# Loading the first half of the first token tile as one DMA, with most constants behind it and the weight loads gated on it

## The chip, the cores and the metric

The kernel runs on the eight cores of one Trainium2 chip; each core computes its own share of the tokens, and the cores do not wait for each other. The metric is the device time of the slowest core in microseconds (us), lower is better. A core's **span** is the time from its first to its last instruction in the trace. Some executions fall into a slower state of the chip, in which the cores of one die (cores 0 to 3 or 4 to 7) show a lower clock; times are compared between fast runs only. The **granted clock** is the share of the TensorE clock that the traces show as let through; "half clock" below means a granted clock of 0.5.

## The reference, cut to what matters

One layer of a decoder: 8 prompts of 2064 tokens (16 of them learned), 128 running sequences with one token each, 1024 channels. The part that matters here is the very beginning: a normalization and a first matrix product.

```python
def rmsnorm(x, g):
    xf = x.astype(jnp.float32)
    y = xf * lax.rsqrt(jnp.mean(xf * xf, axis=-1, keepdims=True) + EPS)
    return (y * g.astype(jnp.float32)).astype(x.dtype)

def trunk_layer(x, ...):
    h = rmsnorm(x, g_pre_mix)
    z = h @ w_in                       # 1024 -> 4096 columns
    u, v, bg, cg, ga, gb = jnp.split(z, IN_SPLITS, axis=-1)
    ...                                # pooling mixer, gated conv mixer, gated FFN
```

## The kernel before: the parts concerned

The tokens of a core are cut into tiles. Channels lie on the partitions: tile 0, called x0, has 8 "rows" of 128 channels by 512 tokens in float32, 256 KB each. The matrix product starts on unnormalized rows (`RAW` = x times the gain), and the normalization factor is multiplied in afterwards; it comes from a sum of squares, which is a matmul with a matrix of equal values (`ONES`). The engines' order is made by a list scheduler from the operations below; `after=` holds a DMA's issue back until another DMA has landed.

```python
def warm(n):                           # fillers: matmuls without a use, they keep the clock up
    pe([(bank(6, 128), ONES, ONES)] * n, [ONESB.t()], [("ps", 6)], 128)

PARTS0 = ((0, 2), (2, 2), (4, 2), (6, 1), (7, 1))          # (first row, rows) of each DMA of x0
for q, (k, m) in enumerate(PARTS0):
    xs0.append(sp_dma(X[0].flat[...], xT[0][k // 2][...], ...))
    if q == 0:
        sp_dma(CST, cst, [], [KCST], 128 * 256 * 4, ...)   # all constants, behind the first piece
...
warm(60)
for i in range(16):
    wload(W_IN, w_in, i, after=[xs0[1 if i else 0]])       # block 0 after piece 0, the others after piece 1
# ... w_pool, w_in 16 to 31, w_co: after=[xs0[1]]
for q in range(4):                                         # tile 1, in four quarters
    pool_dma(X[1].flat[...], xT[1][q], ..., after=[xs0[1]])

for k, m in PARTS0:
    act(... AF.Square ...)                                 # ScalarE: squares of a piece
    for r in range(k, k + m):
        dve(... tensor_scalar, scalar1=cc(C_G1 + k) ...)   # VectorE: RAW, needs the constants
for k, m in PARTS0:
    if k == 6:
        win_group(0, 0, b0, F_lo(0, 0), RAW[0], 0, 6)      # first w_in matmuls, 500 columns
    pe([(bank(SB, N0), ONES, XSQ2[0].ap[:, r, :]) for r in range(k, k + m)], ...)   # sums of squares
    if k < 4:
        warm(20)
# ... five blocks of w_in on tile 0, 512 columns; then tile 1, 392 columns
```

The weight loads (`wload`) and the load of tile 1 are issued by GpSimd, one after the other: eight blocks of w_in, then the four quarters of tile 1, then the next blocks. Each issue takes GpSimd about 0.7 us, the first of a series 0.9.

## Time and profile before

| what | before | from |
|---|---|---|
| time, median of 3 runs | 809.15 us (808.97 to 810.61) | the times |
| span, slowest and fastest core | 809.3 and 806.4 us | cores view |
| TensorE (PE) busy | 98% of the span | profile page |
| first x0 piece (512 KB) lands, mean of 8 cores | 5.20 us | start of the table load on ScalarE |
| tile 1 asked for, mean of 8 cores | 14.39 us | start of GpSimd's `big<-xT` row |
| first scaling of tile 1 by ScalarE, mean | 28.18 us | ScalarE's 128x392 row |
| first matmul on tile 1 (T1), mean and latest | 30.19 and 32.04 us | PE's first 392-column row |

The first line of the profile page:

```profile
span 809.3 us, 15144 instructions; the slowest of 8 cores (806.4 to 809.3 us)
```

PE is the bound, and only its first 60 us differ between cores, so the argument is about the start-up. The next fence is the timeline of core 2, a core that the prediction does not show. Columns: start, length, engine and line, what is read and written, count, and in brackets the idle time before it and what ended that.

```profile
5.24 0.90 POOL L515 DMA_DIRECT2D big<-w_in  x1 [3.89 <-DMA big<-xT]
...
9.77 5.13 POOL L515 DMA_DIRECT2D big<-w_in  x7 [3.63 <-DMA big<-xT]
...
14.89 2.22 POOL L515 DMA_DIRECT2D big<-xT  x4
...
17.70 12.00 PE L502 MATMUL ps<-big 128*128 128x500 bf16 x56 [1.67 <-DMA big<-w_in]
...
28.11 0.59 ACT L694 ACTIVATE big<-ps 128x500 f32<-128x500 f32 x1 [2.34 <-PE ps L502]
...
28.59 0.61 ACT L1049 ACTIVATE big<-big 128x392 bf16<-128x392 f32 x1
```

GpSimd asks for one w_in block when the first piece of x0 has landed, then idles 3.63 us until the second piece has, then asks for seven blocks, and then for tile 1. PE meanwhile waits 1.67 us for block 1. The last two lines are ScalarE's: it first evacuates a block of tile 0 (L694), for which it has waited for PE, and only then scales tile 1 (L1049). PE idles 0.91 to 1.13 us at T1 on every core. This order of ScalarE is the list scheduler's choice.

### The profile page before, as it was taken

Reading aid. Unit: us, or ns where it says so; the run is one execution under the profiler, and the core shown is the slowest. Engines: PE = TensorE matmul, PEld = TensorE weight load, DVE = VectorE, ACT = ScalarE, POOL = GpSimd, SP = SyncE. Lnnn points to the kernel's source line nnn. Section 1 sums busy time; section 2 is a strip of 40 time slices with the busy share of each in tenths; the row PEclk is TensorE's granted clock in tenths of the full one; section 3 lists DMA queues with packets and bytes.
Section 4 is the critical chain, followed back from the end, with each engine's and each line's share of the span. In section 5 each row is a group of like instructions: output and inputs, shape, how many; then the busy total and the mean of one; then the engine's idle time right before and its main releaser. Section 6 shows DMA issues by size and latency. Waiting matters only on the chain.

```text
span 809.3 us, 15144 instructions; the slowest of 8 cores (806.4 to 809.3 us)
## 1 busy us (share of the span) xinstructions
PE 794.6 (98%) x4514; PEld 439.9 (54%) x4518; DVE 557.4 (69%) x971; ACT 431.6 (53%) x813; POOL 251.7 (31%) x268
## 2 busy tenths in 40 slices
PE   6999999999999999999999999999999999999996
PEld 4445445555555555555555555555555555577664
DVE  2897438796986778478899555665567655675656
ACT  3434284765565546576655444644446444565552
POOL 6542002001201133589534321342223422242124
PEclk9999999999999999999999999999999999999999
DMA  9999704756105989997952983382122721159644
GB/s 182 199 164 159 156 1 113 194 151 132 63 23 115 193 150 204 167 162 101 199 163 47 161 170 101 79 157 75 66 77 59 157 80 68 69 103 252 210 154 176
DMA packets 76255, 106.29 MB, mean 131 GB/s; under 512 B 12400, under 2 KB 65776, under 8 KB 76160
## 3 DMA queue, kind: packets, MB, share of 16 engines
q0 software_dynamic: 38992, 43.11, 37.3%
q1 hardware_dynamic: 37184, 62.22, 24.3%
q8 instruction: 39, 0.64, 0.3%
q14 instruction: 40, 0.33, 0.2%
HBM read 106.98 MB, written 28.67 MB: 168 GB/s over the span
## 4 chain that ended last, share of the span: by engine, by line
PE 96%; DMA 2%; DVE 1%; issue 0%; ACT 0%; DVEq 0%; ACTq 0%; POOLq 0%
PE ps L502 96%; DMA big<-w_in 1%; DMA big<-xT 1%; DVE big L582 0%; DVEq L1168 0%; ACT big L1049 0%; DVE big L691 0%; ACT big L570 0%; DVE big L697 0%; ACT big L972 0%; ACT big L954 0%; ACT big L974 0%; ACTq L273 0%; DVE big L978 0%; ACT big L694 0%
## 5 line engine op out<-in xcount | busy, mean ns | idle before, releaser
L502 PE MATMUL ps<-big 128*128 128x392 bf16 (+9 forms) x4514 | 794.6, 339 | 8.1 <-ACT big L1028 2.4
L502 PEld LDWEIGHTS ps<-big 128*128 128x128 bf16 x4518 | 439.9, 98 | 362.5 <-issue 11.9
L856 DVE SCALAR_TENSOR_TENSOR big<-ps,big 128x456 f32<-128x456 f32 (+2 forms) x440 | 268.8, 639 | 103.8 <-ACT big L852 78.9
L870 POOL TENSOR_TENSOR big<-big 128x448 bf16<-128x448 f32 (+2 forms) x110 | 118.5, 1079 | 267.6 <-DVE big L856 165.7
L852 ACT ACTIVATE big<-ps,big 128x448 f32<-128x448 f32 (+2 forms) x220 | 128.9, 599 | 69.4 <-PE ps L502 65.0
L869 ACT ACTIVATE big<-big 128x448 f32<-128x448 f32 (+2 forms) x110 | 60.1, 547 | 52.3 <-DVE big L856 50.7
L733 ACT ACTIVATE big<-ps 128x392 f32<-128x392 f32 (+1 forms) x80 | 39.5, 513 | 58.9 <-PE ps L502 36.2
L513 POOL DMA_DIRECT2D big<-xT x16 | 14.9, 943 | 164.0 <-DVE big L746 150.5
L887 ACT ACTIVATE big<-ps,big 128x448 f32<-128x448 f32 (+1 forms) x32 | 20.4, 637 | 68.2 <-PE ps L502 68.1
L515 POOL DMA_DIRECT2D big<-w_up x44 | 31.9, 726 | 55.0 <-PE ps L502 46.8
L746 DVE SCALAR_TENSOR_TENSOR big<-ps,big 128x392 f32<-128x392 f32 (+1 forms) x40 | 25.8, 645 | 31.9 <-PE ps L502 29.3
L542 DVE TENSOR_TENSOR big<-big 128x1568 bf16<-128x1568 bf16 (+3 forms) x28 | 23.7, 850 | 29.8 <-ACT big L765 29.2
L893 DVE TENSOR_TENSOR big<-big 128x896 bf16<-128x896 bf16 (+1 forms) x12 | 7.6, 630 | 37.2 <-ACT big L890 37.2
L763 ACT ACTIVATE big<-ps,big 128x392 f32<-128x392 f32 (+1 forms) x40 | 24.5, 612 | 14.2 <-PE ps L502 14.1
L639 DVE TENSOR_TENSOR big<-big 128x406 f32<-128x406 f32 (+7 forms) x50 | 29.8, 597 | 1.5 <-ACT big L661 0.2
L582 DVE SCALAR_TENSOR_TENSOR big<-big 128x392 bf16<-128x392 f32 (+1 forms) x40 | 24.2, 645 | 8.1 <-ACT big L559 5.3
L515 POOL DMA_DIRECT2D big<-w_in x32 | 23.2, 752 | 19.3 <-DMA big<-w_in 8.9
L608 ACT ACTIVATE big<-big 128x392 f32<-128x392 f32 (+1 forms) x20 | 12.7, 637 | 29.1 <-DVE big L697 29.1
L817 DVE SCALAR_TENSOR_TENSOR big<-big 128x392 bf16<-128x392 f32 (+1 forms) x40 | 27.1, 710 | 0.8 <-ACT big L556 0.8
L611 DVE SCALAR_TENSOR_TENSOR big<-big 128x392 f32<-128x392 f32 (+1 forms) x40 | 25.4, 641 | 2.6 <-ACT big L608 2.1
L752 DVE TENSOR_TENSOR big<-big 128x392 bf16<-128x392 f32 (+1 forms) x40 | 24.8, 630 | 2.0
L750 DVE TENSOR_TENSOR big<-ps,big 128x392 f32<-128x392 f32 (+1 forms) x40 | 23.3, 583 | 1.9 <-PE ps L502 0.6
(68 smaller groups left out, 345.8 us busy)
## 6 DMA issues: line engine op xcount, KB each, us to landing
big<-w_dnb SPq DMA_DIRECT2D x32, 704.0 KB, 4.6
big<-w_up POOLq DMA_DIRECT2D x44, 256.0 KB, 10.2
big<-w_in POOLq DMA_DIRECT2D x32, 256.0 KB, 22.0
big<-xT POOLq DMA_DIRECT2D x16, 392.0 KB, 6.9
big<-w_dn POOLq DMA_DIRECT2D x8, 704.0 KB, 10.2
w_dnb<-big SPq DMA_DIRECT2D x8, 704.0 KB, 6.4
big<-xT SPq DMA_DIRECT2D x6, 784.0 KB, 6.7
yT<-big SPq DMA_DIRECT2D x6, 784.0 KB, 6.4
```

The costliest lines, as they stand in the source:

```text
L502: ins = e.matmul(o, lhsT=l, rhs=x, start=(start and i == 0), stop=(stop and i == last))
L515: return S.add("pool", lambda e: e.dma_start(out=out, in_=in_, max_dma_last_dim=mx), r, w, dma=True, byts=byts, pri=pri, after=after)
L611: dve(lambda e, k=k: e.scalar_tensor_tensor(out=cv, in0=p[:, 2 + k + lo:2 + k + N], scalar=cc(C_WC + 4 * k + c), in1=cv, op0=ALU.mult, op1 ...
L639: dve(lambda e, nx=nx, cur=cur, s=s, a2=a2: e.tensor_tensor(out=nx[:, a2:W], in0=cur[:, a2:W], in1=cur[:, a2 - s:W - s], op=ALU.add), [ct] ...
L733: act(lambda e, b=b, g=g: e.activation(out=GT[t].ap[:, g, lo:N], in_=bank(b, N, lo), func=AF.Sigmoid), [("ps", b)], [GT[t].t(g, 1)], N, ps ...
L746: dve(lambda e: e.scalar_tensor_tensor(out=A_, in0=bank(bp, N, lo), scalar=cc(C_PS + m), in1=A_, op0=ALU.mult, op1=ALU.mult), [("ps", bp), ...
L752: dve(lambda e: e.tensor_tensor(out=MERGED[t].ap[:, m, lo:N], in0=A_, in1=B_, op=ALU.add), [G_.t(ga, 1), G_.t(gb, 1)], [MERGED[t].t(m, 1)], N)
L817: dve(lambda e: e.scalar_tensor_tensor(out=h, in0=r, scalar=cc(C_G3 + k), in1=SD.ap[:, rs, lo:N], op0=ALU.mult, op1=ALU.mult), [R[t].t(k, ...
L852: act(lambda e, b=b, fj=fj, tt=tt: e.activation(out=tt[:, 0:n], in_=bank(b, n), func=AF.Copy, scale=cc(C_WF + fj)), [("ps", b), KCST], [to ...
L856: dve(lambda e, b=b, fj=fj, tt=tt, k=k: e.scalar_tensor_tensor(out=tt[:, 0:n], in0=ps[:, b * 512 + k:b * 512 + k + n], scalar=cc(C_WF + 44 ...
L869: act(lambda e: e.activation(out=g, in_=g, func=AF.Silu), [T.t(0, 1)], [T.t(0, 1)], N, tab="silu")
L870: S.add("pool", lambda e: e.tensor_tensor(out=gb.ap[:, j, 0:N], in0=g, in1=v, op=ALU.mult), [T.t()], [gb.t(j, 1)], dur=N * 2.17 + 100)
```

## The change

Its intent: fetch x0 in fewer and longer DMAs (four rows, 1 MB, first; contiguous runs of 8 KB instead of 4 KB), let only the 8 constant columns that the start needs go in front and the rest behind, and ask for all weights as soon as that first piece has landed. The fillers between the sums are 10, 10 and 20 in place of 20 and 20, and the length that the list scheduler assumes for the first fillers is set by hand. Cut to its core:

```diff
+PARTS0 = ((0, 4), (4, 2), (6, 2))          # layout of x0 in DRAM
-    PARTS0 = ((0, 2), (2, 2), (4, 2), (6, 1), (7, 1))
-        if q == 0:
-            sp_dma(CST, cst, [], [KCST], 128 * 256 * 4, pri=-2e6 + 2e4)
+    sp_dma(CST[:, 0:8], cst[:, 0:8], [], ["cg1"], 128 * 8 * 4, pri=-2.1e6)
+    LD0 = ((0, 4), (4, 2), (6, 1), (7, 1))
+    for q, (k, m) in enumerate(LD0):
+        xs0.append(sp_dma(X[0].flat[...], x0p[j][...], ...))
+    sp_dma(CST[:, 8:256], cst[:, 8:256], [], [KCST], 128 * 248 * 4, pri=-1.8e6)
...
     for i in range(16):
-        wload(W_IN, w_in, i, after=[xs0[1 if i else 0]])
+        wload(W_IN, w_in, i, after=[xs0[0]])
     # the same for w_pool, w_co, w_o, the other blocks and tile 1: xs0[1] -> xs0[0]
...
-        if k < 4:
-            warm(20)
+            if r < 6:
+                warm(10 if r < 4 else 20)
```

## The prediction

> **What bounds the kernel now.** I read the cores view first, then the timeline of the first 34 us core by core, then the chain of waits, then the windows view for the clock.
>
> ```profile
> core 0: 806.7 us, clock 0.998
> ...
> core 4: 809.3 us, clock 0.997
> core 5: 806.4 us, clock 0.998
> ```
>
> The slowest core sets the time, and the cores differ by 3 us. The windows view says where: from 60 to 800 us PE is busy all the time on every core (200.00 of 200 us in nearly every stretch), so the difference is made before 60 us. In the timelines I take the start of the first matmul group with 392 columns (the second token tile) as a marker, called T1. It is 29.13 us on core 0, 32.04 on core 4, 29.01 on core 5, and 30.65, 30.60, 30.32, 30.43, 29.36 on cores 1, 2, 3, 6, 7. Span minus T1 is 777.6, 777.3, 777.4 for the first three and 777.0 to 777.6 for all eight. So **span = T1 + 777.3 us**, and the change can act on the time only through T1 of the slowest core. Core 4's timeline, PE and ScalarE rows (start, busy time, then in brackets the idle time before and its releaser):
>
> ```profile
> 1.41 5.45 PE L502 MATMUL ps<-big 128*128 128x128 bf16 x60 [1.41 <-POOL big L1011]
> ...
> 5.87 1.28 ACT L1028 ACT_TABLE_LOAD   x1 [5.87 <-DMA big<-xT]
> 7.16 1.06 ACT L1028 ACTIVATE big<-big 128x1024 bf16<-128x1024 f32 x1
> 8.58 3.23 PE L502 MATMUL ps<-big 128*128 128x512 bf16 x43 [1.72 <-ACT big L1028]
> ...
> 12.51 0.59 PE L502 MATMUL ps<-big 128*128 128x512 bf16 x2 [0.70 <-ACT big L1028]
> ...
> 15.33 2.28 PE L502 MATMUL ps<-big 128*128 128x500 bf16 x6 [2.23 <-DMA big<-w_in]
> ...
> 32.04 2.15 PE L502 MATMUL ps<-big 128*128 128x392 bf16 x12 [0.91 <-ACT big L1049]
> ```
>
> PE warms up on 60 fillers, then waits for the squares of x0, then for w_in block 0, which lands at 15.2 us though it was issued at 6.45. The rows of 8 by 512 columns that follow (56 matmuls) take 12.0 us. Then PE idles 0.91 us at T1; on every core it is 0.91 to 1.13 us, because ScalarE scales rows of tile 1 only after it has evacuated a block that PE has just finished. On cores 2, 3, 6 and 7 there is a second DMA wait, for w_in block 1, of 0.9 to 1.7 us. The clock on core 4 (last three columns: granted clock, DMA share, GB/s):
>
> ```profile
> 15.00:15.50 0.50, 0.17 (x1) 0.13 (x2) 0.00 (x0) 0.00 (x0) 0.50 (x2) 1.00 0.95 139
> 15.50:16.00 0.50, 0.50 (x3) 0.23 (x2) 0.00 (x0) 0.00 (x0) 0.50 (x2) 0.75 1.14 158
> 16.00:16.50 0.50, 0.50 (x2) 0.15 (x1) 0.00 (x0) 0.00 (x0) 0.50 (x2) 0.50 1.08 174
> ...
> 19.00:19.50 0.50, 0.50 (x3) 0.24 (x2) 0.00 (x0) 0.41 (x2) 0.50 (x1) 0.84 1.16 176
> ```
>
> Read the clock column: half speed from about 15.75 (0.75 is half of the slice) to 19.16 us, 3.4 us in all, which costs 1.7 us of matmul time. Core 1 has the same from about 14.25 to 17.05. The other six have none. So core 4 is slowest because its w_in block came last and because it was throttled.
>
> **What the skill says.** The Trainium skill, "TensorE: Matmul & The Clock Gate", Part 1, describes a gate that halves the PE clock after an idle window of about 3.4 us, free-running against the kernel. The length agrees with the 3.41 us above. The trigger is looser here: the window before core 4's drop (12.33 to 15.75) held 0.59 + 0.42 us of PE work, 30%; the one before core 1's held about 42%. On core 7 a window with about 51% did not trip it. I work with "under half busy". The skill, "ScalarE: Activation LUTs", What ACT_TABLE_LOAD costs, gives 1283 ns; the trace has 1.28 us, and it starts only when the first x0 piece has landed. The skill, "Perfetto Trace Analysis", DMA Optimizations, says that growing small DMA runs to 4 or 8 KB raises throughput. This trace cannot show 8 KB, but it shows a dip: on core 4 115 GB/s in the half microsecond after 6.0 us, between 332 and 215, about when the constants in 1 KB rows pass; every core has one. The skill, "DMA: Bandwidth & Descriptors", Specifications, says that pieces below 512 B are read, modified and written. That bears on the new 32-byte rows of constants; no row of this trace shows it.
>
> **The change part by part.**
>
> x0 pieces. Before: 512 KB first, landing at 4.66 to 5.87 us over the cores, 1.18 MB (with the constants) at 7.5 to 9.5. After: a 4 KB piece, then 1.05 MB as one DMA. The extra issue costs 0.43 us (mean issue time in the timeline). Summing the GB/s column, 1.05 MB had moved by 5.6 to 6.95 us, the constants' dip in it. Take 0.4 for the dip off and 0.43 for the issue on, add the lag from moved to landed (0.5 to 1.4 us on the first piece, 1.0 to 2.6 on the second): the piece A of four rows **lands at about 7.6 us**, 7.0 to 8.5.
>
> First square. It now waits for A. Table load 1.28 + square 1.06 + 0.15 of semaphores: first sum matmul at 7.6 + 2.5 = 10.1 us, against 8.58 on core 4 and about 7.4 to 8.0 on the others. Fillers end at 6.33 to 7.68 (1.41 plus 4.92 to 6.27). So the first PE gap **grows from about 1.1 to about 3 us**. That is my chosen point of danger: nearly every position of a 3.4 us window over such a gap has a window under half busy (core 4's 5.7 to 9.1 would hold 1.2 us, 35%).
>
> Fillers and sums at half clock. A sum pair of 512 columns takes 0.86 us instead of 0.43, ten fillers 1.07 instead of 0.56. From 10.1: pair 10.96, ten 12.03, pair 12.9, ten 13.96, pair 14.8, twenty at most 17.0. The clock returns after a window full of work, between 13.1 and 16.5 by the core's phase, so the last part runs fast: **the first w_in matmul starts at 15.1 to 16.7 us** (before: 13.2 to 15.3). At full clock it would be 13.75.
>
> w_in block 0. Issued at A + 0.6, with 0.9 for the first issue, so it enters at 9.1 us with some 0.3 to 0.5 MB of x0 and constants before it. It reads 0.52 MB at about 320 GB/s (the column shows about 160 GB/s written as bf16, half the bytes read), so 1.6 + 1.3 + about 2 of lag: about 14. Block 1 follows some 1.7 us later, ahead of its use, so the second DMA wait of cores 2, 3, 6 and 7 goes.
>
> To T1. From the first w_in matmul: 6 matmuls, the last two sums and 2 matmuls 2.2 us at full clock, 56 matmuls 12.0, idle 0.91: 15.1 us. So T1 = 30.2 to 31.8, slowest core about 31.4 against 32.04. There is a floor: the second quarter of tile 1 lands at about 28 us (ScalarE picks it up at 28.26 to 28.38 on the fast cores), its scaling makes T1 about 29.0. Bytes ahead of it are unchanged, so it stays near 28.
>
> Constants. The remaining ones land at 11 to 11.5 us, first needed for the logarithm's bias after 15 us: no cost. Sum: 0.6 us less on the slowest core, **808.7 us** by 777.3 + 31.4; I take reported time and slowest span as equal (809.15 and 809.3).
>
> **The rivals.** First: the intended gain. If A lands early, or PE is not throttled in the gap, the first w_in matmul starts when block 0 lands, at 13.8 to 14.3 us, with no wait for block 1 and no half clock later. T1 is then 29.0 to 29.8, the last by the floor, and the time about 806.9. For it: every part removes a wait that some core shows, and x0 no longer shares the DMA engines with w_in. Against: the gap above. Second: the throttle lasts longer. On a core whose phase makes the half clock last to 16.5 us and whose A lands after 8.2, the whole sequence moves to 17.5 us and T1 to 32.6 or more: about 810. For it: eight cores with free phases make the worst case likely on one of them. Third: the DMA stream is the limit in any case; T1 of cores 0 and 5 already sits at its floor of 29.0, so nothing below 806.3 can be had without loading tile 1 earlier.
>
> **Range and chances.** Weights of 0.55 for the main line (808.7), 0.3 for the intended gain (806.9) and 0.15 for the longer throttle (810) give 808.4. The runs before lie over 1.6 us by themselves. I predict **808.4 us, range 806.5 to 810.2**. Two per cent are 16 us, more than the whole start-up that can be affected, so within 2% has 0.98 and each side 0.01.
>
> **What would show it right or wrong.** Right: the table load starts at 7.0 to 8.5 us; the PE gap after the 60 fillers is 2.5 to 3.5 us; the clock column falls to 0.5 on most cores between 8 and 12 us and is back at 1.0 by 17; no PE wait for w_in block 1; span minus T1 still 777.3 within 0.4. Wrong, towards faster: the clock stays at 1.0 through the gap, and the first w_in matmul waits for its DMA at 13.5 to 14.5. Wrong, towards slower: T1 above 32.5 on some core, or a DMA wait for tile 1 in front of T1, which would mean that the stream got slower. If span minus T1 moves by more than 0.5, the scheduler has reordered something later and my one-marker account fails.

## More of the kernel before

Stretches of 1 us on core 1, from the windows view; the last three columns are the granted clock of PE, the DMA share and GB/s (a packet is counted whole in the stretch where it starts, so a share can be over 1):

```profile
3.00:4.00 1.00, 1.00 (x12) 1.00 (x11) 0.00 (x0) 0.00 (x0) 0.00 (x0) 1.00 0.72 221
4.00:5.00 1.00, 1.00 (x13) 1.00 (x11) 0.00 (x0) 0.00 (x0) 0.00 (x0) 1.00 0.92 343
...
12.00:13.00 1.00, 0.59 (x2) 0.13 (x2) 0.78 (x3) 1.00 (x3) 1.00 (x2) 1.00 1.21 192
13.00:14.00 1.00, 0.06 (x1) 0.09 (x2) 0.20 (x1) 0.33 (x1) 1.00 (x2) 1.00 1.16 179
```

The DMA engines are busy in all four of them (these stretches answer to those shown of the changed kernel below).

## The result, and the profile after

The four runs after took 812.05, 810.82, 895.97 and 864.37 us. The last two are in the slow state (a die at clock 0.89 to 0.96). Executions in which one die ran at a lower clock are left out of the means. The kernel before, its three runs with a fourth taken beside these, had a median of 809.48 us (808.97 to 810.61). The ratio of fast runs is 1.0022 with a 95% interval of 0.9998 to 1.0046: the same within 2%, and rather slower than faster. Ratios here are the mean time of one kernel's fast runs over that of the other's in the same rounds, so not quite the ratio of the medians that are quoted. Both fast runs lie above the predicted 808.4 us and above the upper end of the range, 810.2 us.

Cores view after:

```profile
core 0: 807.7 us, clock 0.997
core 1: 810.5 us, clock 0.994
...
core 4: 809.3 us, clock 0.993
```

Core 1 is now the slowest, and both it and core 4 have a lower clock than any core before. The timeline of core 1:

```profile
1.41 5.39 PE L504 MATMUL ps<-big 128*128 128x128 bf16 x60 [1.41 <-POOL big L1019]
...
10.22 1.28 ACT L1039 ACT_TABLE_LOAD   x1 [10.22 <-DMA big<-x0a]
10.80 6.04 POOL L517 DMA_DIRECT2D big<-w_in  x8 [9.45 <-DMA big<-x0a]
...
12.71 10.59 PE L504 MATMUL ps<-big 128*128 128x512 bf16 x72 [5.91 <-ACT big L1039]
16.81 2.24 POOL L517 DMA_DIRECT2D big<-xT  x4
...
24.53 8.63 PE L504 MATMUL ps<-big 128*128 128x500 bf16 x40 [1.24 <-DMA big<-w_in]
...
31.25 0.62 ACT L1062 ACTIVATE big<-big 128x392 bf16<-128x392 f32 x1 [1.52 <-DMA big<-xT]
...
33.42 2.81 PE L504 MATMUL ps<-big 128*128 128x392 bf16 x16 [0.26 <-ACT big L1062]
```

The 1 MB piece lands at 10.22 us. PE has run out of fillers at 6.80 and waits 5.91 us for the first square. GpSimd asks for the first weights at 10.80 and for tile 1 at 16.81. Before T1, which is 33.42 us here, ScalarE waits 1.52 us for tile 1 to land. The chain of waits of the same core names the same pieces (start, length, what):

```profile
1.51 8.63 DMA big<-x0a
...
10.80 6.01 POOL big L517 x8
16.81 14.36 DMA big<-xT
```

Loading x0, issuing eight weight loads and fetching tile 1 follow each other without slack. The windows view of core 1:

```profile
3.00:4.00 1.00, 1.00 (x12) 1.00 (x11) 0.00 (x0) 0.00 (x0) 0.00 (x0) 1.00 1.20 106
4.00:5.00 1.00, 1.00 (x13) 1.00 (x11) 0.00 (x0) 0.00 (x0) 0.00 (x0) 1.00 0.49 123
...
9.00:10.00 1.00, 0.00 (x0) 0.00 (x0) 0.00 (x0) 0.00 (x0) 0.00 (x0) 0.50 0.90 246
...
12.00:13.00 1.00, 0.29 (x1) 0.14 (x2) 1.00 (x3) 1.00 (x2) 1.00 (x2) 0.50 0.11 38
13.00:14.00 1.00, 1.00 (x7) 0.63 (x6) 0.51 (x3) 1.00 (x2) 1.00 (x3) 0.50 0.55 25
14.00:15.00 1.00, 1.00 (x9) 0.74 (x7) 0.00 (x0) 1.00 (x3) 1.00 (x2) 0.50 0.90 137
```

Two things are to be seen. The clock is at half speed, from 8.81 to 15.63 us in finer slices. And what the DMA engines move has two holes: 106 and 123 GB/s at 3 to 5 us, where the kernel before had 221 and 343, and 38 and 25 GB/s at 12 to 14 us, where it had 192 and 179. In the first hole the engines are not idle: the share is 1.20 at 3 to 4 us, which is 19.2 us of packet time on 16 engines for the 13 packets of 8 KB that 106 GB/s make in 1 us: 1.5 us for each. All eight cores have it (49 to 262 GB/s at 3 to 4 us, before 221 to 403). The second is core 1's own: the last piece of x0 lands at 12.78 us and the weights were asked for too late to be moving yet; the other seven cores had 89 to 202 GB/s there.

All eight cores side by side (means of the eight, from the timelines of the profiled runs):

| | before | after |
|---|---|---|
| first x0 piece lands | 5.20 (4.66 to 5.87) | 8.73 (8.31 to 10.22) |
| first w_in block asked for | 5.78 | 9.32 |
| block 1 asked for | 9.29 | 10.20 |
| tile 1 asked for | 14.39 | 15.31 |
| first quarter of tile 1 lands | 27.30 | 28.98 |
| first scaling of tile 1 | 28.18 | 29.08 |
| PE idle at T1 | 0.96 (0.91 to 1.13) | 0.30 (0.00 to 0.73) |
| T1 | 30.19 (29.01 to 32.04) | 31.33 (30.46 to 33.42) |
| cores with half clock | 2, 3.4 us each | 8; 3.4 us on six, 6.8 us on cores 1 and 4 |
| span minus T1 | 777.0 to 777.6 | 777.06 to 777.71 |

The earlier request did not come about: the gate opens on a piece that lands as late as the second piece did before. Since block 0 now stands behind the gate too, GpSimd has eight issues and not seven between the gate and tile 1, and tile 1 is asked for 0.92 us later (15.31 less 14.39). It is scaled 0.90 us later, and T1 is 1.14 us later.

### The profile page after: what moved, and what is told of

The parts are those of the page before. It is cut to its first block, busy times and chain, and to the rows that moved or that the text cites. A ratio compares the mean times of both kernels' runs of the same rounds, so it can differ in the third digit from the quotient of the medians.

```text
span 810.5 us, 15151 instructions; the slowest of 8 cores (807.7 to 810.5 us)
## 1 busy us (share of the span) xinstructions
PE 794.5 (98%) x4518; PEld 440.2 (54%) x4518; DVE 556.8 (69%) x971; ACT 432.3 (53%) x813; POOL 251.6 (31%) x268
## 4 chain that ended last, share of the span: by engine, by line
PE 94%; DMA 3%; POOL 1%; DVE 1%; issue 0%; ACT 0%; DVEq 0%; SPq 0%; ACTq 0%; POOLq 0%
PE ps L504 94%; DMA big<-xT 2%; DMA big<-x0a 1%; POOL big L517 1%; DVE big L584 0%; DVEq L1181 0%; ACT big L1062 0%; DVE big L693 0%; ACT big L572 0%; DVE big L699 0%; SPq L511 0%; ACT big L979 0%; ACT big L961 0%; ACT big L981 0%; ACTq L274 0%
## 5 line engine op out<-in xcount | busy, mean ns | idle before, releaser
L504 PE MATMUL ps<-big 128*128 128x392 bf16 (+8 forms) x4518 | 794.5, 339 | 9.6 <-ACT big L1039 5.9
L515 POOL DMA_DIRECT2D big<-xT x12 | 10.5, 884 | 97.4 <-DVE big L748 85.8
L584 DVE SCALAR_TENSOR_TENSOR big<-big 128x392 bf16<-128x392 f32 (+1 forms) x40 | 24.2, 645 | 8.8 <-ACT big L561 7.6
```

Of the source, the lines that this page charges most:

```text
L504: ins = e.matmul(o, lhsT=l, rhs=x, start=(start and i == 0), stop=(stop and i == last))
```

## The experiments

All eighteen runs gave correct results (seventeen kernels: e13 is e10 once more). Beside the ratio to the kernel before I use the **mean span**, over all cores and all fast runs of a kernel: it has less noise than the time, which is that of the slowest core. Between the fast runs of one kernel the mean of the eight cores still varies by 0.3 to 1.1 us, so that differences of 0.3 us are not resolved. The kernel before had 807.4 to 807.7 us in every set of runs, the changed one 808.42 (two runs).

An edit can also move the order that the list scheduler gives to ScalarE and VectorE. By the traces, the order up to T1 is that of the kernel started from in e1, e3, e5, e7, e8, e11, in e9 and f1 but for the added square, and in e12 but for two swapped squares. In e2, e4 and f2 it moved among tile 1's first rows. In e6, e10, e13, f3, f4 and f6, which start from the kernel before, the scaling of tile 1 moved in front of the evacuation, as in the change; f3 moved further.

| kernel | ratio of fast runs, 95% | mean span |
|---|---|---|
| e1_fill | 1.0020 (1.0004 to 1.0036) | 808.70 |
| e2_gate | 1.0008 (0.9988 to 1.0028) | 808.85 |
| e3_split | 1.0020 (1.0006 to 1.0035) | 809.27 |
| e4_both | 1.0006 (0.9989 to 1.0023) | 808.13 |
| e5_cglate | 1.0001 (0.9982 to 1.0021) | 807.38 |
| e6_bcst | 1.0004 (0.9988 to 1.0021) | 807.37 |
| e7_oldlay | 1.0016 (1.0001 to 1.0031) | 809.01 |
| e8_wide | 1.0012 (0.9996 to 1.0029) | 808.61 |
| e9_btab | 0.9999 (0.9984 to 1.0014) | 807.58 |
| e10_bgate | 0.9981 (0.9963 to 0.9999) | 806.20 |
| e11_cgpool | 0.9993 (0.9978 to 1.0008) | 807.35 |
| e12_row7 | 1.0027 (1.0012 to 1.0043) | 809.43 |
| e13_gate_again | 0.9974 (0.9960 to 0.9988) | 806.39 |
| f1_three | 0.9994 (0.9981 to 1.0006) | 807.21 |
| f2_half | 0.9993 (0.9980 to 1.0006) | 807.31 |
| f3_gatefill | 0.9996 (0.9984 to 1.0009) | 807.48 |
| f4_gatefill0 | 0.9982 (0.9969 to 0.9996) | 806.68 |
| f6_cst2 | 0.9975 (0.9960 to 0.9990) | 806.41 |

My theory was that the PE gap and the half clock it brings ate the gain. The rivals were that the size of the first piece delays the request for the weights, so that the DMA stream sets T1, and that the load of x0 itself had become slower.

### Is it the clock? More fillers

The changed kernel with twice the fillers at the start:

```diff
-    warm(60)
+    warm(120)
```

> Changed kernel with 120 warm-up fillers instead of 60, nothing else. Two theories of what sets T1 (start of the first 392-column group; 30.5 to 33.4 us in the changed kernel). Clock theory: the PE gap in front of the first sum matmul (3.3 to 5.9 us) halves the clock; with the gap filled, the clock stays at 1.0 on at least 6 of 8 cores, the first w_in matmul starts at 13.8 to 14.8 us instead of 15.9 to 17.7, and T1 falls by 1 us or more on most cores. Stream theory: the blocks and tile 1 arrive later because nothing of them is asked for before 1 MB of x0 has landed; then the clock is cured but T1 falls by less than 0.5 us, and PE waits for a DMA or for the scaling of tile 1 instead.

The half clock of the start-up was gone on seven of eight cores (core 3 had it later, at 20.8 to 24.2 us). The time was 811.82 us, the ratio to the kernel before 1.0020: no gain over the change. The timeline of core 5:

```profile
1.41 8.77 PE L504 MATMUL ps<-big 128*128 128x128 bf16 x120 [1.41 <-POOL big L1019]
...
29.65 0.62 ACT L1062 ACTIVATE big<-big 128x392 bf16<-128x392 f32 x1 [1.74 <-DMA big<-xT]
...
32.02 2.15 PE L504 MATMUL ps<-big 128*128 128x392 bf16 x12 [1.72 <-ACT big L1062]
```

PE now arrives early at tile 1 and idles 1.72 us, behind a ScalarE that had waited 1.74 us for its DMA. T1 is 30.98 us in the mean, against 31.33. So the half clock is real, but its cost lies beside a DMA wait: my first theory fell as the one cause. The two limits lie close together in the changed kernel: on cores 4 and 6 the first scaling waited for no DMA there, and PE idled only 0.30 us at T1 in the mean.

### Is it the size of the piece? Splitting it again

Three variants of the changed kernel load rows 0 to 3 in two halves:

```diff
-    LD0 = ((0, 4), (4, 2), (6, 1), (7, 1))
+    LD0 = ((0, 2), (2, 2), (4, 2), (6, 1), (7, 1))
```

In e2_gate the requests wait for the first half only, and the squares still for both (`after=[xs0[1]]` on the square, so that only the requests move):

> Changed kernel with the first x0 piece loaded as two halves from the same tensor; w_in and tile 1 are released by the first half, but the first square still waits for the second half. Stream theory: the first w_in issue moves from 8.9 to about 6 us, tile 1's first rows are there 0.5 to 1.5 us earlier, T1 falls by about 1 us. Clock theory: the gap in front of the first sum stays over 3 us (or grows, as w_in now shares the DMA with x0), the clock is halved on most cores, first w_in matmul still near 16 us or later, T1 within 0.5 us of the changed kernel or worse.

In e3_split the squares follow each half, and the requests wait for both halves (`after=[xs0[1]]` on every load):

> Changed kernel with the first x0 piece loaded as two halves, each squared as it lands; w_in and tile 1 are still released only when both halves (1 MB) have landed. Clock theory: the table load starts at 5.0 to 6.3 us, the first PE gap shrinks to under 1.5 us, the clock stays at 1.0 on most cores, first w_in matmul at about 14, T1 lower by 1 us or more on most cores. Stream theory: T1 lower by less than 0.5 us. Side question, 8 KB against 4 KB runs with the same bytes: if the long runs made the piece slow, the second half lands at about 7.6 us instead of 8.3 to 10.2, and the first w_in issue comes that much earlier; if not, it lands at 8.3 or later.

In e4_both squares and requests both follow the first half:

> Changed kernel with the first x0 piece loaded as two halves, each squared as it lands, and w_in and tile 1 released by the first half: both suspected losses undone, the constants still behind x0 and the fillers still short. If clock and stream together are the loss: first w_in matmul at 13 to 14.5 us, no half clock on most cores, T1 29 to 30.5 on all, slowest span about 1 to 2 us under the changed kernel and level with the kernel before or 0.5 us under it. If neither is the loss, T1 stays at 30.5 to 33.4.

Measured: mean spans of 808.85, 809.27 and 808.13 us, against 808.42 for the change. Neither half of the split pays by itself; together they bring 0.3 us, hardly more than the noise, and not the time of the kernel before. The half clock stayed on all eight cores in e2 and e4. In e2 PE itself became the limit: the second half came later (the first square's table load started at 9.39 us, not 8.73), the half clock lasted 6.8 us on six cores, and though tile 1 was asked for 1.5 us earlier (13.79), its first scaling waited for no DMA on six cores and T1 was 32.08 us in the mean. The first half landed at 7.2 to 8.4 us in e4, though before it was the same 512 KB landing at 4.66 to 5.87. That pointed to the third theory: the load of x0 itself is slower, and the only thing new in front of it are the 8 constant columns, 4 KB.

### Is it the DMA in front?

Here the 8 columns are issued behind the 1 MB piece (the rest of the change is kept):

```diff
-    sp_dma(CST[:, 0:8], cst[:, 0:8], [], ["cg1"], 128 * 8 * 4, pri=-2.1e6)
+    sp_dma(CST[:, 0:8], cst[:, 0:8], [], ["cg1"], 128 * 8 * 4, pri=-1.98e6)
```

> Changed kernel with the 4 KB DMA of the first eight constant columns (32-byte rows) issued after the 1 MB piece of x0 instead of before it. In the changed kernel and the four runs so far, the first x0 piece lands late (1 MB at 7.8 to 10.2 us, and even half of it at 7.2 to 8.4 in three quarters of the cores, against 4.7 to 5.9 for half in the kernel before), and the moved GB/s fall to 0 to 200 between 3.5 and 5 us on all cores. Theory constants: the small rows in front of x0 stall the DMA engines; then the 1 MB piece lands at 6.8 to 7.8 us here and the hole at 3.5 to 5 us goes or moves behind it; first PE gap 2.3 to 3.3 us, still half clock on most cores, T1 lower by 0.5 to 1 us on average (31.34 in the changed kernel). Theory size or layout: landing stays at 8.0 us or later.

The piece landed at 7.45 us in the mean, not 8.73; the mean span fell by 1.04 us, to 807.38; half clock was left on five cores. The windows view of core 1:

```profile
3.00:4.00 1.00, 1.00 (x12) 1.00 (x11) 0.00 (x0) 0.00 (x0) 0.00 (x0) 1.00 0.88 295
4.00:5.00 1.00, 1.00 (x13) 1.00 (x11) 0.00 (x0) 0.00 (x0) 0.00 (x0) 1.00 1.11 352
```

The first hole is gone: 295 and 352 GB/s where the changed kernel had 106 and 123. By the share of 0.88, a packet of 8 KB took 0.4 us here and 1.5 there. The issue in front costs 0.45 us (from 1.06 to 1.51 in the timeline), so 0.83 of the 1.28 us are lost in another way.

The reverse, the kernel before with only its constants treated as in the change:

```diff
+    sp_dma(CST[:, 0:8], cst[:, 0:8], [], ["cg1"], 128 * 8 * 4, pri=-2.1e6)
-        if q == 0:
-            sp_dma(CST, cst, [], [KCST], 128 * 256 * 4, pri=-2e6 + 2e4)
+    sp_dma(CST[:, 8:256], cst[:, 8:256], [], [KCST], 128 * 248 * 4, pri=-1.8e6)
```

> Kernel before with only the constants changed as in the change: eight columns first, the rest behind x0; all else (x0 layout, pieces, gates, fillers) as before. Theory constants: the first 512 KB piece lands at 6.5 us or later on most cores instead of 4.7 to 5.9, the hole at 3.5 to 5 us appears, the first sums come at 9 us or later, the clock is halved on more cores than the two of the kernel before, and the mean T1 (30.19 before) rises by 0.5 us or more. Theory size or layout: the first piece lands at 5.1 to 6.3 (0.43 later for the issue), no hole, T1 as before or a little lower because the constants' 1 KB rows no longer sit between the pieces.

The first 512 KB landed at 6.55 us, not 5.20: 1.35 later, 0.90 beyond the issue. The mechanism shows here too, and half clock came on six cores. Yet the mean span did not move (807.37 against 807.49). Most weights wait for the second piece in that kernel, and tile 1 was asked for at 14.23 us, no later than before; so it may be that the DMA in front costs time only where the requests hang on the first piece. This run does not show it: the order of ScalarE moved too (PE idle at T1 0.61 us, not 0.96), which may have paid for a loss.

What makes it expensive? Three variants of the changed kernel. With 128 columns in front, so that its rows have 512 bytes and not 32 (cut: the rest of the constants then starts at column 128):

```diff
-    sp_dma(CST[:, 0:8], cst[:, 0:8], [], ["cg1"], 128 * 8 * 4, pri=-2.1e6)
+    sp_dma(CST[:, 0:128], cst[:, 0:128], [], ["cg1"], 128 * 128 * 4, pri=-2.1e6)
```

> Changed kernel with the constants still first, but 128 columns of them (512-byte rows, 64 KB) instead of 8 (32-byte rows, 4 KB). If it is the 32-byte rows that stall the DMA engines: no hole at 3.5 to 5 us, 1 MB landing at 7.0 to 8.4 us (0.2 us for 64 KB, against 8.3 to 10.2). If any DMA in front does it: landing at 8.3 us or later, with the hole.

The piece landed at 8.76 us (8.73 with 8 columns), and the hole stayed. The short rows are not the cause.

With the 8 columns issued by GpSimd, on its own queue (`pool_dma` in place of `sp_dma`):

> Changed kernel with the DMA of the eight constant columns issued from GpSimd's queue instead of in front of x0 on the sync engine's queue. If being in front on the same queue is the cost: 1 MB lands at 6.6 to 8.2 us as with the constants behind it, mean span over the cores about 1.0 us below the changed kernel. If the constants' transfer itself disturbs the DMA engines: landing at 8.0 or later, mean span as the changed kernel. (The fillers start about 0.7 us later, because the same engine writes the ones that they multiply.)

It landed at 7.86 us, without the hole; mean span 807.35. Off the queue of x0 the DMA costs 0.4 us and not 1.3.

With the constants behind the piece, and a row of x0 in front of it, 256 KB in 2 KB runs:

```diff
+        ... pri=-2e6 + 4e4 * q - (2e5 if q == 3 else 0)     # row 7 is issued first
```

> Changed kernel with the last 256 KB piece of x0 (one row) put in front of the 1 MB piece, and the eight constant columns behind it. Bytes alone would make the 1 MB land 0.8 us later than with nothing in front (6.6 to 8.6), so at 7.4 to 9.4. If any DMA in front costs about 1 us beyond its bytes and issue: 8.6 to 10.4 us, with a hole in the moved GB/s at 3.5 to 5 us. If only the constants do that: 7.4 to 9.2 and no hole.

The 1 MB piece landed at 9.43 us, 1.98 later than in e5. The bytes account for about 0.8 (my estimate: 262,144 bytes at the 330 GB/s that the windows show) and the issue for 0.45; 0.7 us are left. So 4 KB, 64 KB and 256 KB in front all cost 0.7 to 0.9 us beyond issue and bytes. That this is so is shown three ways. Why it is so stays open: the views show packets of 8 KB that take 1.5 us and not 0.4, but not what they wait for.

### Is it the longer runs?

The changed kernel with x0 in its old layout, the same 1 MB fetched in runs of 4 KB:

```diff
+        if m == 4:
+            o_, i_ = X[0].flat[:, 0:4 * N0].rearrange("p (c n) -> p c n", c=2), xT[0][0:2].rearrange("c p n -> p c n")
```

> Changed kernel with x0 in the old layout: the same 1 MB in the first DMA, but as 4 KB runs from two blocks; constants still first. Theory constants: landing of the 1 MB at 8 us or later as in the changed kernel, hole still there, T1 mean within 0.6 of 31.34. Theory size or layout: landing at 6.8 to 7.8 us.

It landed at 8.69 us against 8.73: runs of 8 KB neither help nor hurt. (Its mean span of 809.01 is within what two fast runs of the changed kernel leave open.)

### What is the gate worth by itself?

First a control that is independent of the DMAs, the kernel before with ScalarE's table loaded early, by a square of 8 columns at the start:

```diff
+    act(lambda e: e.activation(out=SD.ap[:, 2, 0:8], in_=ONES[:, 0:8], func=AF.Square), [ONESB.t()], [SD.t(2, 1)], 8)
```

> Kernel before with one 8-column square of a constant on ScalarE at the very start, so that the 1.28 us table load is over before x0 lands. First sums 1.2 us earlier (6.2 to 7.4 us), the PE gap after the fillers nearly gone. As the first w_in matmul waits for its DMA at 13.2 to 15.4 us anyway, I expect T1 unchanged on cores without half clock (29.0 to 30.7); a core with less PE work in the window before 14 to 16 us may even be throttled more often. Time within 0.1% of before.

The first sums came at 6.1 to 7.3 us in place of 7.4 to 8.6, and the mean span was 807.58: nothing gained. Starting PE's first real work earlier is worth nothing while the weights and tile 1 come no earlier.

Then the gates alone: the kernel before, all its weight loads and tile 1 waiting for the first 512 KB only. The pieces, the constants and the fillers stay.

```diff
-        wload(W_IN, w_in, i, after=[xs0[1 if i else 0]])
+        wload(W_IN, w_in, i, after=[xs0[0]])
     # and xs0[1] -> xs0[0] for all others, with tile 1 and w_o
```

> Kernel before with only the gates changed: every w_in block and tile 1 released by the first 512 KB piece instead of block 0 by the first and the rest by the second. If the gate alone helps: no PE wait for w_in block 1 (0.9 to 1.7 us on four cores before), T1 mean down by 0.3 to 0.8 us from 30.19. If earlier w_in only takes bandwidth from x0: the last x0 piece lands later than 13 to 14 us, the first w_in matmul or the sums come later, T1 the same or up.

The median of the four fast runs was 808.68 us against 810.98, the ratio 0.9981, the mean span 806.20 against 807.42. Core 2, whose lines of before are shown above:

```profile
5.45 5.99 POOL L515 DMA_DIRECT2D big<-w_in  x8 [4.10 <-DMA big<-xT]
...
11.44 2.21 POOL L515 DMA_DIRECT2D big<-xT  x4
...
13.49 14.21 PE L502 MATMUL ps<-big 128*128 128x500 bf16 x66 [1.73 <-DMA big<-w_in]
...
26.15 0.62 ACT L1049 ACTIVATE big<-big 128x392 bf16<-128x392 f32 x1 [0.64 <-DMA big<-xT]
...
28.37 13.96 PE L502 MATMUL ps<-big 128*128 128x392 bf16 x74 [0.67 <-ACT big L1049]
...
31.56 0.56 ACT L694 ACTIVATE big<-ps 128x500 f32<-128x500 f32 x1
```

GpSimd's wait of 3.63 us between block 0 and block 1 is gone, tile 1 is asked for at 11.44 and not 14.89 us, PE no longer stops for block 1, and T1 is 28.37 in place of 30.60. But the last line shows that not only the gate moved: the evacuation (L694), in front of the scaling of tile 1 before, now comes behind it, and PE idles 0.28 us at T1 in the mean, not 0.96. With the old 0.96 T1 would be 29.7 us in the mean and not 29.03, by adding the difference, against 30.19 before: an estimate by which the order has about half of the gain. No run has the new gates with the old order, so the two are not told apart. Two cores of this run:

```profile
core 2: 805.1 us, clock 0.998
core 3: 806.7 us, clock 0.996
```

A second set of runs, on another chip, with the same kernel:

> The same kernel as the early gates alone, on this call's chip, for comparison and to see if it holds. If its gain is real: mean span 806.0 to 806.6 against 807.4 for the kernel before, ratio 0.9975 to 0.9990. If it was luck of one chip: ratio over 0.9995.

Ratio 0.9974, mean span 806.39 against 807.67. With the whole constants moved behind the second piece as well (`if q == 1` in place of `if q == 0`):

> Early gates, with the constants' DMA (whole, 1 KB rows) one place later: behind the second 512 KB piece instead of behind the first. If what follows the first piece in the queue delays it: first landing at 5.6 to 7.0 us instead of 4.7 to 5.9, first w_in matmul about 0.5 us later, mean span 0.3 to 0.8 us over the gate alone. If not (so it was the layout with 8 KB rows in the changed kernel): landing 4.7 to 5.9, mean span the same within 0.3 us.

Ratio 0.9975, mean span 806.41: the same as the gate alone. The first piece landed at 5.20 us in the mean, the same as before, so what follows the first piece does not delay it.

### Can the versions be improved?

f1_three is the changed kernel with the constants behind the piece, 90 fillers and the early table load:

> Changed kernel with the three losses mended together: the eight constant columns behind the 1 MB piece (as in the run that showed it landing 1 us earlier), an 8-column square at the start so that the table load is over before x0 lands, and 90 fillers instead of 60. If small rows, table load and clock together are the loss: 1 MB lands at 6.6 to 8.6 us, first sums 1.2 us after it (7.8 to 9.8), no half clock on at least 6 cores, first w_in matmul at 13 to 15.5, T1 28.4 to 30.5, mean about 29.4; time 0.1 to 0.2% under the kernel before. If the stream of w_in and tile 1 sets T1 whatever PE does: T1 as in the run with only the constants moved (mean 30.0), time level with before.

Half clock was left on core 4 before T1, and came on core 5 at 29.65 us. The mean span was 807.21, against 807.38 with the constants alone (e5): fillers and table load add next to nothing.

f2_half is the same with x0's first rows in halves, the gate on the first half and 70 fillers:

> As the three mends together, but the 1 MB as two halves, each squared as it lands, w_in and tile 1 released by the first half (constants' eight columns behind the second, 70 fillers). First half lands at 4.7 to 5.9 us as before; w_in is asked for at 5.3 to 6.5 instead of 7.2 to 9.2. If the time at which w_in is asked for sets T1: first w_in matmul at 12.5 to 14.5, T1 mean 0.3 to 0.8 us under the version with the whole 1 MB. If the DMA engines are simply full from 2 to 28 us: T1 the same within 0.3 us, as the same bytes must pass.

The mean span was 807.31 us, worse than the gate on the kernel before, though tile 1 was asked for at 12.70 us. The trace shows a part of the reason: on cores 3 and 6 the half clock lasted 6.8 us, the first scaling of tile 1 waited for no DMA, and T1 came at 31.39 and 31.53 us, against 28.40 to 30.31 on the other six. I cannot say what takes the rest.

f3_gatefill is e10_bgate with 20 more fillers after the third pair of rows (`if k < 6` in place of `if k < 4`), to take the half clock away that two cores of e10 still had:

> Kernel before with the gates of the change (everything released by the first 512 KB piece) and twenty more fillers after the third pair of sums. The early gate alone gave a mean T1 of 29.0 and half clock on two cores from about 14 to 18 us. If that half clock costs: none here, T1 28.3 to 29.3 on all cores, slowest span 0.3 to 0.7 us below the gate alone. If the stream of tile 1 is the floor anyway: same within 0.3 us. Either way 0.15 to 0.25% under the kernel before.

There was no half clock any more, and the mean span was 807.48: the whole gain was gone. The cause is seen after T1. Core 2 of f3_gatefill:

```profile
41.14 3.53 PE L502 MATMUL ps<-big 128*128 128x500 bf16 x16 [1.89 <-DVE big L691]
```

and core 2 of e10_bgate at the corresponding place:

```profile
42.86 7.38 PE L502 MATMUL ps<-big 128*128 128x392 bf16 x39 [0.54 <-DVE big L691]
```

The list scheduler had ordered ScalarE and VectorE differently, since it reckons with the fillers' time, and PE waits 1.89 us for VectorE. Span minus T1 is 777.8 to 778.9 in place of 776.8 to 777.1. So f3 says nothing of the clock. f4_gatefill0 puts the question again with the order kept: 40 fillers after the second pair, with the scheduler's duration left at that of 20.

```diff
-            warm(20)
+            warm(20 + 10 * k)
+            last_pe[0].dur = 20 * (128 / 2.4 + 1.5)
```

> Kernel before with the early gates and 40 instead of 20 fillers after the second pair of sums, the length that the list scheduler assumes left as it was, so every engine's order is that of the early gates alone. If the half clock on some cores costs: none here, slowest span 0.3 to 0.8 us under the gate alone, span minus T1 at 776.9. If not: same within 0.3 us.

Half clock on one core, ratio 0.9982, mean span 806.68: no gain over the gate alone (806.39 on the same chip). That does not clear the half clock: it went from two cores (e13) to one. In the profiled runs of e10, e13, f4 and f6 the nine cores with half clock have a T1 of 29.77 us in the mean and the other 23 of 29.24, and on eight of the nine the first scaling of tile 1 waited for no DMA. Whether the half clock made them late or came with a late block 0 is not shown.

### What the runs say together

Each line has means of the eight cores in the profiled run:

| kernel | tile 1 asked for | first scaling of tile 1 | span | span minus scaling |
|---|---|---|---|---|
| e10_bgate | 11.82 | 26.83 | 805.99 | 779.2 |
| f6_cst2 | 11.88 | 27.08 | 806.05 | 779.0 |
| e13_gate_again | 11.79 | 27.46 | 806.61 | 779.2 |
| e5_cglate | 14.05 | 27.54 | 807.34 | 779.8 |
| before | 14.39 | 28.18 | 807.48 | 779.3 |
| after | 15.31 | 29.08 | 808.61 | 779.5 |
| e1_fill | 15.25 | 28.48 | 808.65 | 780.2 |
| e2_gate | 13.79 | 29.31 | 809.08 | 779.8 |
| f3_gatefill | 11.78 | 26.81 | 807.64 | 780.8 |
| e12_row7 | 16.10 | 29.58 | 809.56 | 780.0 |
| e3_split | 16.21 | 30.09 | 809.45 | 779.4 |

The later tile 1 is asked for, the later it is scaled, by and large, and the span goes along with that: the last column stays within 1.2 us while the span moves by 3.6, f3 left aside. The nine runs not shown fit the first part (asked for at 11.93 to 15.32 us, scaled at 27.19 to 29.19). e2 breaks it: there PE came later than tile 1. f3 breaks the second part, by its order. Where PE's clock was repaired (e1) the span did not come earlier. The table is a correlation; that it is a wait and no coincidence is seen in the timelines, where the releaser of that scaling is `DMA big<-xT` on most cores after the change (six of eight), on none before, and on five with the gate alone. In e10 the requests come 2.57 us earlier than before, but the first quarter of tile 1 lands only 0.67 earlier (26.63, not 27.30), and before the change ScalarE waited for it on no core. So most of the 1.35 us by which its scaling comes earlier is not tile 1's: it is ScalarE's order, and the wait for a second w_in block that is gone (0.65 to 1.67 us on five cores before, none in e10). After the change it is tile 1's: it lands at 28.98 and is scaled at 29.08.

So the balance of the change is: the gate, with the order of ScalarE that came with it, is worth about -1.2 us of mean span (e10 and e13); the DMA in front of the first piece costs about 1.0 (changed kernel less e5); what is left against e10, about 1.1 (e5 less e10 and e13), belongs to the later landing of a piece of twice the size, with the later square and request that follow. The last term is a remainder and not a measurement, it holds the other edits of the change too, and the terms do not simply add in other combinations, as e6 and f2 show.

The best version is the gate alone (with f6, which is level with it). It was 0.19% and 0.26% faster than the kernel before on two chips, and its mean span is 2 us below that of the changed kernel.

## Why the prediction was wrong, and where it was right

**Span = T1 + 777.3** held: 777.06 to 777.71 on the eight cores. It is an account for one order of instructions only, as the prediction said: f3_gatefill broke it.

**"I take reported time and slowest span as equal"** was a mis-sized term. In the profiled run before, the time was 810.78 us and the slowest span 809.3; in every fast run the reported time is 1.5 to 1.7 us above the slowest span. I had put a median beside the span of another run. This is 1.5 of the 3.0 us by which the fast runs' mean, 811.4, missed.

**"The piece A of four rows lands at about 7.6 us"** failed: 8.73 in the mean, 10.22 on core 1, and three cores outside 7.0 to 8.5. The adding up of the bytes was good to 0.3 us: without the 0.43 for the issue it gives 7.2, and e5_cglate, which has no DMA in front, landed at 7.45. The term that was missing is the DMA in front, of which I had counted the issue of 0.43 us alone; it costs 0.83 us more. The dip that I put down to the constants was misread: on core 4 nine tenths of their 1 KB packets had started by 5.6 us, at 283 to 332 GB/s, and the dip is at 6.0.

**"The first PE gap grows from about 1.1 to about 3 us"** had the right mechanism and was too small: 3.3 to 5.9 us. The half clock that it was to bring came on all eight cores. The first w_in matmul came at 15.82 to 17.64 us, against 15.1 to 16.7 predicted: six cores inside, cores 1 and 4 outside. These two had the half clock for two windows, 6.8 us, as in the second rival, "the throttle lasts longer": T1 at 33.42 and 32.24. Core 4 fits it, but for a DMA wait of 0.28 us. Core 1, the slowest, does not: its scaling of tile 1 waited 1.52 us for the DMA. So it is luck that this rival's "about 810", with the 1.5 us of the term above, comes to the 811.4 that was measured. I had given it a weight of 0.15, and twice that to the intended gain, of which no core showed anything.

**"Bytes ahead of it are unchanged, so it stays near 28"**, said of the second quarter of tile 1, is the step that failed in substance: that quarter landed at 29.17 to 32.46 us, where it had landed at 27.74 to 29.18. The bytes are unchanged, but not the time at which tile 1 is asked for: with eight issues behind the gate it moved from 14.39 to 15.31 us, on core 1 to 16.81, and the first scaling from 28.18 to 29.08, on core 1 to 31.25. I treated the floor under T1 as fixed and looked for the damage in the clock; e1_fill shows that the floor had risen so far that a mended clock gained nothing.

**"Idle 0.91" at T1** was carried over, and did not hold: with the new order of ScalarE it was 0.00 to 0.73 us. So the 15.1 us from the first w_in matmul to T1 came out at 14.3 to 15.8, a sum that held with a term that did not.

**"No PE wait for w_in block 1"**: five cores (2, 3, 5, 6 and 7) had a second wait for w_in before, of 0.65 to 1.67 us; after, three (1, 2 and 5) have a wait for a later block, of 0.3 to 1.2 us. The signs named for "wrong, towards slower" were both there: T1 above 32.5 on core 1, and a DMA wait for tile 1 in front of T1.

**The third rival**, that the DMA stream is the limit and nothing below 806.3 can be had without loading tile 1 earlier, was right in part. After the change the stream is the limit on most cores, and e10_bgate, which loads tile 1 earlier, has a mean span of 806.2, where the variants that do not stay at 807.2 or more. But 29.0 was no floor: before, ScalarE waited for tile 1 on no core, and T1 was 27.78 on core 2 of f1_three (span 805.1) and 28.39 on core 4 of e5_cglate (805.7), which ask for it no earlier than the earliest core before (13.36 and 13.22 us, against 13.21). And 806.3 was meant for the slowest core: in e10's fast runs that is 807.5 in the mean.

**The slowest core.** The mean T1 of 31.33 lay inside the predicted 30.2 to 31.8 us. But the time is the latest of eight, and I set it to 31.4; it was 33.42. Main line 808.7, plus 2.0 for T1, less 0.2 for span minus T1 (777.10 on core 1), plus 1.5 for the offset, is 812.0: the profiled run, 812.05. The range was too narrow for a maximum over eight cores.

**The constants** that moved back were free, as said. **Within 2%** was right.

## What to carry to other kernels

Ask of every gated load when its request goes out, and count the issues that stand between the gate and the load that is needed last: a gate on an earlier event that is itself made later gains nothing. In these runs such a gate did best on a small first piece with nothing in front of it in its queue, not even 4 KB. When an edit changes what a scheduler knows, compare the engines' orders in the traces before you give the gain to the edit. When you predict the slowest of eight cores, predict a maximum, and check how the reported time relates to the span that you work with.

## What the Trainium skill lacked or had wrong

- "TensorE: Matmul & The Clock Gate", Part 1: the length of the window agrees (3.41 us of half clock, or 6.8 for two windows). Its trigger, an idle window, is too strict. In the first 35 us of all cores of the 20 profiled runs, cut into windows of 3.41 us that start where the trace's clock records do, the clock fell after 85 windows, which held up to 45% of PE work (84 of them under 43%), and stayed after 1257, none of which held less than 42%. So the border lies near 43%, a little lower than the "under half busy" of the prediction, for these traces at least. And half clock need not cost time: with it gone on seven of eight cores of e1_fill the kernel was as slow (ratio to before 1.0020) as with it on all eight (1.0022).
- "DMA: Bandwidth & Descriptors", Specifications, on pieces under 512 bytes: rows of 32 bytes and of 512 bytes in front of the 1 MB piece made it land at 8.73 and 8.76 us, so that rule does not explain the loss.
- "DMA: Bandwidth & Descriptors", Bandwidth, gives 0.68 us for a DMA of 4 KB and 0.95 for one of 64 KB by itself, issued from GpSimd; no run here shows whether that is what is lost. It does not say that a small DMA in front delays a large one of the same queue by 0.7 to 0.9 us beyond its issue and bytes (5.20 to 6.55 and 7.45 to 8.73 us with 4 KB, 7.45 to 9.43 with 256 KB). Of issuing from another engine it says that this saves only the issue time; here it saved 0.87 us (8.73 to 7.86), of which the issue is 0.45.
- "Perfetto Trace Analysis", DMA Optimizations, speaks of batching transfers of about 2 KB into 4 or 8 KB; on the step from 4 KB to 8 KB it is silent. Here that step changed nothing (8.69 and 8.73 us for 1 MB).
- No page that I read says how the reported time relates to the span of the slowest core: it is 1.5 to 1.7 us more in every fast run.
